# Hybrid S5 and sparse-attention decoder step on one core: layer 1's compression page loads start after layer 0's attention output projection, yields between the key splits, and other ScalarE and GpSimd costs in the emission's model

## The chip, the cores and the metric

One Trainium2 chip, and one of its cores. The time is device microseconds of one execution of the whole program. A profiled execution gives, beside its time, the span from the first to the last instruction and the records of every engine: PE (TensorE matmuls), PEld (TensorE weight loads), DVE (VectorE), ACT (ScalarE), POOL (GpSimd) and SP (SyncE, which issues the DMAs here).

## The reference

Two layers of a parallel-branch trunk work on 512 prompt tokens and on 32 sample tokens (8 sequences of 4), all in float32, D = 1024. Each layer does this:

- modulation: `mod = silu(c) @ ada_w + ada_b`, three parts, `h = rmsnorm(x) * (1 + scale) + shift`;
- one input projection `h @ w_in`, split into the S5 branch, the queries, six key and value groups, gates and merge logits;
- an S5 state-space scan, GELU, a gated linear unit and an output projection;
- sparse attention in three parts. The *compressed* part turns blocks of 64 key or value rows into one row, `silu(blk @ w1) @ w2`; for the sample tokens these rows lie in 128 pages of a paged cache (8 sequences of 16 pages) and have to be fetched by a page table. The *selected* part attends to the best blocks, the *window* part to the last 512 rows;
- `b_nsa = (o * silu(z_nsa)) @ w_nsa_out`, the two branches merged by sigmoid gates, `out = merged @ w_o`, `x = x + gate * out`.

After the second layer one RMSNorm gives the outputs. Layer 1 can't be modulated before layer 0's `x` is complete, but its cache pages and its modulation weights depend on the inputs alone.

## The kernel before

**Arithmetic.** Each big product runs as three matmuls on float32r halves: an operand is split into a rounded copy (`act.copy`, a CAST on ScalarE) and the rest (`sub`, a subtraction on VectorE). A weight tile of 128 x 1024 is fetched by one 512 KB DMA through a ring of three buffers, cast, subtracted and used. One projection of 128 outputs takes 48 matmuls (8 blocks of the input, 3 products, 2 halves of the tokens), one with 512 inputs takes 24.

**Emission.** The program is written as some dozen Python generators (`dense`, `compress`, `prompt`, `sample`, `s5`, `modulation`, page loaders and so on). A scheduler (`_Sched.run`, line 252) picks one of them at each step, lets it emit a few instructions and takes the next; nothing is reordered afterwards. Every engine then executes its own instructions in the order of emission, so an instruction that has to wait holds back all that stand behind it on that engine. The scheduler goes by a model of the engines (`_Clock.note`, line 146), which adds up a cost for each instruction and remembers when each piece of memory is written and read. The model's time of TensorE is the scheduler's clock. A generator yields a delay, a wait for a named event (`ev`), for room in memory, or for the modelled time at which operands are ready. Among those that are ready the lowest number wins: page loaders 4, sample attention 5, compression 15, prompt attention 20, modulation 25, dense 50. So a matmul of the compression goes ahead of the dense work as soon as the *model* holds its pages to be landed.

**ScalarE and GpSimd in the model** (lines 204 to 211). A ScalarE instruction costs 0.051 us where an operand is in PSUM, else 0.093, plus 0.83 ns for each element of a row, plus 0.09 for an accumulator and 0.09 for a bias operand. The same sum is the time for which the engine is held and the time at which its result is visible. A GpSimd operation other than a copy or memset costs 0.27 us plus 2.7 ns an element.

**Between the layers.** When layer 0's attention is complete (event `att`), several generators go on at once:

- `dense` (lines 1103 to 1122) does the attention's output projection, here called *nsa*: eight tiles m of 24 matmuls. Each half tile is merged on VectorE with two spilled arrays, `mn` and `mt`, which `gates(m)` fetches two tiles ahead through three buffers. Then comes the output projection *wo*: eight tiles of 48 matmuls, each with its weight DMA (`in_wo`) and a DMA of old x (`in_xT`), and the root-mean-square of the new x. With event `x` the layer is complete, its normalisation and layer 1's `modulate` follow, and `dense` of layer 1.
- `compress(1)` (line 1612) takes its memory, fetches `cw2`, `cw1` (2 of 1 MB) and `pe4`, and spawns `loads()` (line 1639), which fetches the 128 pages in eight chunks c0 to c7, four pages at a time, 128 KB each (`in_cmp`). There are two chunk buffers: the pages of chunk c wait for the products of chunk c-2. `products` of a chunk are 128 matmuls. From c5 on they wait for event `x` (CMP_LATE = 5), and c7 also for layer 1's own keys.
- `modulation` of layer 1 fetches 24 tiles of `ada_w` of 512 KB in pairs, each pair after the matmuls of the last.

All of these DMAs are issued by SP, in the order of emission.

**Key splits.** `prompt` (line 1705) starts, in each layer, when the input projection and the new compressed rows are there. It first splits the keys: four times a CAST of 64 x 512 and a subtraction of 64 x 512 (lines 1730 to 1734), without a yield between them.

Of the kernel before, what the change touches and what calls it, by code (L numbers as in the profile page):

```python
# [18 lines left out]
PSUM = bass.MemoryType.PSUM  # L19
# [84 lines left out]
class _Clock:  # L104
# [41 lines left out]
    def note(self, e, op, args, kw):  # L146

        named = dict(kw)
        views = [x for x in args if isinstance(x, bass.AP)] + [x for x in named.values() if isinstance(x, bass.AP)]
        if not views:  # L150
            return 0.0
        out = named.get("out", views[0])
        outs = [out] + ([named["accum_out"]] if "accum_out" in named else [])
        ins = [x for x in views if not any(x is y for y in outs)]
        rs, wr = [self.span(x) for x in ins], [self.span(x) for x in outs if not x.tensor.name.startswith("out_")]
        data = max([x[0, c].max() for x, c in rs], default=0.0)
        room = max(x[0 if e != "pe" else 1:, c].max() for x, c in wr) if wr else 0.0
        n = max(x.free_size() for x in views)
        t0 = self.free.get(e, 0.0)
        t0 = max(t0, data + 0.13, room + 0.13 if room > t0 else 0.0)  # L160
        if e == "pe":

            n, rhs, p0 = out.free_size(), views[-1] if op == "matmul" else views[1], out.offset // out.ap[0][0]
            wide = rhs.dtype == F32
            m, k_, r0 = out.ap[0][1], views[1].ap[0][1], views[1].offset // views[1].ap[0][0]
            up = lambda x: 1 if x <= 32 else 2 if x <= 64 else 4
            tile_, passes = (up(k_), up(m)), 2 if wide and op == "matmul" else 1
            load = (0.045 if rhs.dtype == BF16 else 0.111) * up(m) / 4  # L170
            c = 2 * n / 2400 + 0.003 if wide else n / (2400 if rhs.dtype == BF16 else 2180) + 0.002
            if not self.warm(t0):
                c, load = 2 * c, 2 * load
            ready = max(data + 0.15, room + 0.15)
            qs = {(r, q) for r in range(r0 // 32, r0 // 32 + up(k_)) for q in range(p0 // 32, p0 // 32 + up(m))}
            k = int(max(self.free[e], ready) // TICK)
            if passes == 2 and tile_ == self.tile and not qs & self.quads and ready <= self.begun + 0.05:
                self.quads |= qs
                end = self.free[e] + 0.007
            else:  # L180
                if tile_ == self.tile:
                    t0 = max(self.free[e], load + max(self.pass0, ready))
                else:
                    t0 = load + max(self.free[e] + (0.09 if self.tile else 0.0), ready)
                c = max(c, load)
                self.quads, self.tile, self.begun = qs, tile_, t0
                end, self.pass0 = t0 + passes * c, t0 + (passes - 1) * c
            self.ticks[k] = self.ticks.get(k, 0) + n * k_ / P * (1 if not wide else 4 if op == "matmul" else 2)
            self.free[e] = end
            vis = end + 0.07  # L190
        elif op == "dma_start":
            h = self.free[e] = t0 + 0.45
            d = max(self.free.get("dma", 0.0), h + 0.65)
            n = max(x.free_size() * x.ap[0][1] for x in views[:2]) / P if out.space != DRAM else out.free_size() * out.ap[0][1] / P
            end = self.free["dma"] = d + n * 1.42e-3 + 0.01
            vis = end + 0.78
        else:
            extra = 0.061 * sum(1 for x in ins[1:] if x.free_size() == 1) if e == "dve" else 0.0
            if e == "dve":
                far = any(abs(x.ap[-1][0]) >= 8 and x.ap[-1][1] > 1 for x in ins)  # L200
                fast = op in ("tensor_scalar", "tensor_copy", "memset") and all(x.space != PSUM for x in [out] + ins)
                c = 0.155 + extra + n * (0.0063 if op == "reciprocal" else 0.0019 if op == "tensor_tensor_scan" else
                                         0.00055 if fast else 0.0015 if far else 0.001)
            elif e == "act":
                table = {AF.Sin: "sin", AF.Sqrt: "sqrt", AF.Tanh: "exp", AF.Exp: "exp"}.get(args[2] if len(args) > 2 else None)
                if table and table != self.table:
                    t0, self.table = t0 + 1.28, table
                c = (0.051 if any(x.space == PSUM for x in ins) else 0.093) + n * 0.00083 + 0.09 * (
                    ("accum_out" in named) + (isinstance(named.get("bias"), bass.AP)))
            else:  # L210
                c = 0.27 + n * (0.0035 if op == "tensor_copy" else 0.0009 if op == "memset" else 0.0027)
            vis = end = self.free[e] = t0 + c
        for x, c in rs:
            x[1, c] = np.maximum(x[1, c], end)
        for x, c in wr:
            x[0, c] = np.maximum(x[0, c], vis)
        return vis
# [75 lines left out]
def body(ctx: ExitStack, tc: tile.TileContext, A, O):  # L293
# [52 lines left out]
    def t(lat=0.0):  # L346
        return ("t", lat)
# [3 lines left out]
    def ev(*k):  # L351
        return ("ev", k)

    def done(*k):
        S.events[k] = S.ready
# [155 lines left out]
    def sub(dst_lo, src, hi):  # L511
        dve.tensor_tensor(dst_lo, src, hi.bitcast(F32), op=ALU.subtract)
# [13 lines left out]
    def unlag():  # L526
        while lagged:
            sub(*lagged.pop())
# [226 lines left out]
    def dense(l):  # L755
# [352 lines left out]
        for m2 in range(4):  # L1108
            w = wnext(("nsaow", l, m2))
            for m in (2 * m2, 2 * m2 + 1):  # L1110
# [3 lines left out]
                for h, (a, b) in enumerate(HALVES):  # L1114
# [5 lines left out]
                    split_lag(mh(m, a, b), ml(m, a, b), mt(m, a, b))  # L1120
                    yield t()
        unlag()
        for b in mnb:
            b.free()
        for b in q["ogh"] + [q["ogb"]]:
# [440 lines left out]
    def page_ids(i, n=4):  # L1566
        S.clock.free["sp"] = max(S.clock.free.get("sp", 0.0), S.now) + 0.3 + 0.11 * n
        _, v = nc.values_load_multi_w_load_instructions(
            pt[0:1, i:i + n], engines=[mybir.EngineType.SP], min_val=0, max_val=A["cmp"].shape[0] - 1,
            skip_runtime_bounds_check_because="the page table is clamped to the pool on chip")  # L1570
        return v
# [40 lines left out]
    def compress(l):  # L1612
# [24 lines left out]
        done("ckb", l)  # L1637

        def loads():
            for c in range(NB):  # L1640
                if c >= CKB[l]:
                    yield ev("ck", l, c - CKB[l])
                ck = cks[c % CKB[l]]
                for i in range(0, NPG, 4):
                    for j, v in enumerate(page_ids(NPG * c + i)):
                        sp.dma_start(ck[:, i + j].rearrange("p t d c -> p (t d c)"),
                                     A["cmp"][ds(v, 1), l].rearrange("g p f -> (g p) f"))
                    yield t(PG_LAT)
                yield "for", [], [ck[:, 0:NPG + 1]]
                yield t(CK_LATE)  # L1650
                done("ckl", l, c)
        S.spawn(loads(), 4, "ckload")
        if l > 0:
            yield ev("att", l - 1)
        for c in range(NB):
# [15 lines left out]
            n = 84 if last else 64  # L1671
# [33 lines left out]
    def prompt(l):  # L1705
# [24 lines left out]
        for at in range(2):  # L1730
            for g in range(2):
                src = qk(4 + at)[half[g], 0:T]
                act.copy(ks[at][g][half[g]], src)
                sub(ks[at][g][half[1 - g]], src, ks[at][g][half[g]])
            q["qkb"][4 + at].free()

        def queries(qt, r):
# [350 lines left out]
    def main():  # L2088
# [4 lines left out]
        S.spawn(modulation_first([B[6], B[4]]), 2, "ada0")  # L2093
        S.spawn(modulate(0), 3, "h")
        S.spawn(dense(0), 50, "dense")
        yield ev("modq", 0)
        sp.dma_start(pt, A["page_table"])
# [19 lines left out]
        for l in range(DEPTH):  # L2117
            yield ev("qkv", l)
            S.spawn(prompt(l), PR_PRIO, "prompt")
            yield ev("gelu", l, 3)  # L2120
            S.spawn(sample(l), SM_PRIO, "sample")
            if l + 1 < DEPTH:
                yield ev("att", l)
                S.spawn(compress(l + 1), CMP_PRIO, "cmp")
# [229 lines left out]
```

## Time and profile before

| | |
|---|---|
| runs of the kernel | 1247.3 us median of 3 (1238.85 to 1257.79) |
| profiled execution | 1244.75 us |
| its span | 1243.0 us, mean granted TensorE clock 0.967 |
| PE busy | 1142.0 us, 92% |
| PEld busy | 1037.6 us, 83% |
| DVE busy | 780.4 us, 63% |
| ACT busy | 481.5 us, 39% |
| POOL busy | 154.8 us, 12% |
| chain that ended last | PE 69%, DMA 11%, DVE 7%, ACT 4%, SP queue 4% |

Engines work side by side, so the busy shares don't add up. The granted clock is 1 at 2.4 GHz and 0.5 at 1.2 GHz; a mean between them says for how much of a stretch TensorE ran at the lower level. Layer 0 goes up to about 660 us, layer 1 from there.

### The profile page before, as it was taken

The numbers are of one execution on the slowest core, as the hardware profiler recorded it, in microseconds if no ns is written. First come the engines' busy times: TensorE is split into PE (matmuls) and PEld (weight loads), VectorE is DVE, ScalarE is ACT, GpSimd is POOL, SyncE is SP. The second block draws the span as 40 slices with busy tenths as digits, with TensorE's granted clock in tenths as the row PEclk, the third lists the DMA queues.
The fourth block names the chain that finished last, engine by engine and source line by source line (L and its number), as shares of the span: only waits on it lengthen the run. The fifth ranks groups of instructions, "written<-read, shape, count | busy, mean of one in ns | idle before, by whom it ended". The sixth has DMA issues, their size and how long they took to land.

```text
span 1243.0 us, 30351 instructions
## 1 busy us (share of the span) xinstructions
PE 1142.0 (92%) x11702; PEld 1037.6 (83%) x11702; DVE 780.4 (63%) x1787; ACT 481.5 (39%) x1130; POOL 154.8 (12%) x335
## 2 busy tenths in 40 slices
PE   4989999999999999887897999979999899999995
PEld 3788999988888888777885899868898788889995
DVE  4766777566666755763336587797665667556854
ACT  4432432333444444432125233244343444454332
POOL 0122261010000000000002033450010000000001
PEclk9999999999999999988998999989999999999997
DMA  9575666657567655349998744545466665733742
GB/s 386 218 225 180 192 181 187 180 176 245 153 187 237 190 165 170 107 165 294 308 308 262 268 162 133 160 135 142 129 213 197 197 194 167 235 104 97 237 131 81
DMA packets 174434, 239.19 MB, mean 192 GB/s; under 512 B 33233, under 2 KB 129618, under 8 KB 172498
## 3 DMA queue, kind: packets, MB, share of 16 engines
q1 hardware_dynamic: 174290, 237.25, 60.2%
q8 instruction: 92, 1.51, 0.5%
q14 instruction: 52, 0.43, 0.1%
HBM read 207.53 MB, written 37.98 MB: 198 GB/s over the span
## 4 chain that ended last, share of the span: by engine, by line
PE 69%; DMA 11%; DVE 7%; ACT 4%; SPq 4%; issue 2%; POOL 0%; DVEq 0%; ACTq 0%; POOLq 0%
PE bank L231 69%; DVE m L231 7%; SPq L231 3%; ACT m L231 3%; DMA m<-in_cmp 2%; DMA m<-in_cw 2%; DMA yd<-m 1%; DMA m<-in_ada_w 1%; DMA m<-kpd 1%; DMA m<-ud 1%; DMA m<-yd 1%; DMA m<-in_s5k 0%; DMA m<-in_wo 0%; ACT L231 0%; DMA gd<-m 0%
## 5 line engine op out<-in xcount | busy, mean ns | idle before, releaser
L231 PE MATMUL bank<-m,m 128*128 128x256 f32 (+13 forms) x10540 | 1048.2, 283 | 62.5 <-DVE m L231 26.6
L231 PEld LDWEIGHTS bank<-m,m 128*128 128x128 f32 (+4 forms) x10540 | 946.5, 168 | 135.5 <-issue 55.4
L231 DVE TENSOR_TENSOR m<-m,m 128x1024 fp32r<-128x1024 f32 (+15 forms) x635 | 386.2, 630 | 156.8 <-ACT m L231 129.6
L231 ACT CAST m<-m 128x1024 fp32r<-128x1024 f32 (+5 forms) x274 | 174.2, 650 | 89.3 <-DVE m L231 62.8
L231 ACT COPY m<-bank 128x512 f32<-128x512 f32 (+7 forms) x258 | 100.1, 400 | 268.0 <-PE bank L231 258.4
L231 ACT ACTIVATE m<-m 128x544 f32<-128x544 f32 (+8 forms) x74 | 34.7, 476 | 186.0 <-DVE m L231 171.8
L231 POOL TENSOR_TENSOR m<-m,m 128x32 f32<-128x32 f32 (+4 forms) x100 | 57.6, 595 | 327.3 <-DMA x_mid<-m 152.8
L231 PE MATMUL bank<-c_k,m 128*128 128x128 f32 (+2 forms) x590 | 88.8, 277 | 5.0 <-DVE m L231 2.8
L231 ACT ACTIVATE m<-bank 128x288 f32<-128x288 f32 (+4 forms) x130 | 50.4, 390 | 104.5 <-PE bank L231 103.8
L231 POOL CAST m<-m 64x128 fp32r<-64x128 f32 x64 | 23.3, 364 | 505.2 <-ACT m L231 426.5
L231 PEld LDWEIGHTS bank<-c_k,m 128*128 128x128 f32 (+1 forms) x590 | 68.0, 145 | 15.0 <-DVE m L231 5.2
L231 ACT ACTIVATE m<-bank,m 128x128 f32<-128x128 f32 (+4 forms) x132 | 67.8, 523 | 14.4 <-DVE m L231 11.4
L231 DVE TENSOR_REDUCE m<-bank 128x1 f32<-128x128 f32 (+4 forms) x132 | 57.3, 474 | 18.6 <-PE bank L231 17.9
L231 DVE COPY m<-bank 128x32 f32<-128x32 f32 (+6 forms) x102 | 39.1, 389 | 46.4 <-ACT m L231 24.7
L231 DVE SCALAR_TENSOR_TENSOR m<-m,bank 128x256 f32<-128x256 f32 x96 | 41.5, 434 | 41.2 <-ACT m L231 25.1
L231 POOL TENSOR_TENSOR m<-m,c_k 128x256 f32<-128x256 f32 (+2 forms) x32 | 36.0, 1126 | 158.8 <-PE bank L231 136.1
L231 DVE TENSOR_SCALAR m<-m,m,m 128x128 f32<-128x128 f32 (+3 forms) x132 | 52.5, 439 | 2.5
L231 DVE SCALAR_TENSOR_TENSOR m<-m,m 128x64 f32<-128x64 f32 (+5 forms) x64 | 28.9, 480 | 18.5 <-ACT m L231 18.0
L231 ACT ACTIVATE m<-m,m 128x512 f32<-128x512 f32 (+2 forms) x24 | 15.9, 662 | 59.9 <-DVE m L231 59.9
L231 DVE SCALAR_TENSOR_TENSOR m<-bank,mod,m 128x256 f32<-128x256 f32 x32 | 15.4, 482 | 34.9 <-PE bank L231 21.3
L231 DVE TENSOR_TENSOR m<-bank,m 64x16 f32<-64x16 f32 (+1 forms) x56 | 19.8, 385 | 24.4 <-PE bank L231 23.4
L231 ACT ACT_TABLE_LOAD x24 | 30.8, 1283 | 7.1 <-DVE m L231 6.0
(59 smaller groups left out, 397.2 us busy)
## 6 DMA issues: line engine op xcount, KB each, us to landing
m<-in_wblk SPq DMA_DIRECT2D x78, 512.0 KB, 4.1
m<-in_cmp SPq DMA_DIRECT2D x256, 128.0 KB, 3.7
m<-in_kvsel SPq DMA_DIRECT2D x256, 128.0 KB, 3.0
m<-in_ada_w SPq DMA_DIRECT2D x32, 512.0 KB, 5.1
m<-in_ada_q SPq DMA_DIRECT2D x8, 1024.0 KB, 14.7
m<-in_wo SPq DMA_DIRECT2D x16, 512.0 KB, 4.8
ms<-m SPq DMA_DIRECT2D x16, 272.0 KB, 3.3
m<-ms SPq DMA_DIRECT2D x16, 272.0 KB, 3.4
```

The source lines that it names most:

```text
L231: return f(*args, **kw)
```

## The change

The model charges ScalarE 0.074 us more for an instruction with an operand in PSUM and 0.052 us more for any other, and GpSimd 0.4 ns more an element. `dense` sets an event `nsa` when it has emitted the attention's output projection, and the page loader of layer 1 waits for that event of layer 0 ahead of its first page. The four key splits of `prompt` yield 0.4 us after each. No instruction is added, taken out or changed in shape; only the order of emission can differ.

```diff
@@ _Clock.note
-                c = (0.051 if any(x.space == PSUM for x in ins) else 0.093) + n * 0.00083 + 0.09 * (
+                c = (0.125 if any(x.space == PSUM for x in ins) else 0.145) + n * 0.00083 + 0.09 * (
                     ("accum_out" in named) + (isinstance(named.get("bias"), bass.AP)))
             else:
-                c = 0.27 + n * (0.0035 if op == "tensor_copy" else 0.0009 if op == "memset" else 0.0027)
+                c = 0.27 + n * (0.0035 if op == "tensor_copy" else 0.0009 if op == "memset" else 0.0031)
@@ dense
         unlag()
+        done("nsa", l)
         for b in mnb:
             b.free()
@@ compress
         def loads():
+            if l > 0:
+                yield ev("nsa", l - 1)
             for c in range(NB):
@@ prompt
                 act.copy(ks[at][g][half[g]], src)
                 sub(ks[at][g][half[1 - g]], src, ks[at][g][half[g]])
+                yield t(0.4)
             q["qkb"][4 + at].free()
```

## Rows read from the trace of the kernel before

**Rows 1.** The page: busy us, share of the span and instructions of each engine.

```profile
PE 1142.0 (92%) x11702; PEld 1037.6 (83%) x11702; DVE 780.4 (63%) x1787; ACT 481.5 (39%) x1130; POOL 154.8 (12%) x335
```

**Rows 2.** Table of stretches: stretch, its us, busy us (instructions) by engine, clock, DMA, GB/s.

```profile
536.00:700.00 164.00, 138.71 (x1754) 126.97 (x1755) 75.87 (x186) 46.14 (x93) 6.46 (x22) 0.91 0.86 283
557.00:575.00 18.00, 9.66 (x70) 8.71 (x64) 5.83 (x14) 2.62 (x5) 0.00 (x0) 0.81 0.88 287
660.00:700.00 40.00, 29.57 (x401) 26.04 (x402) 22.14 (x65) 16.70 (x40) 6.46 (x22) 0.79 0.82 271
```

**Rows 3.** Timeline of PE after layer 0's attention: start, us, instructions, [idle before, releaser].

```profile
564.81 5.37 PE L231 MATMUL bank<-m,m 128*128 128x256 f32 x24 [5.14 <-DVE m L231]
570.93 1.68 PE L231 MATMUL bank<-m,m 128*128 128x256 f32 x12 [0.75 <-DVE m L231]
574.56 7.21 PE L231 MATMUL bank<-m,m 128*64 128x68 f32 x152 [1.95 <-DMA m<-in_cmp]
595.30 6.45 PE L231 MATMUL bank<-m,m 128*64 128x64 f32 x146 [3.29 <-DMA m<-in_cmp]
...
685.00 8.80 PE L231 MATMUL bank<-m,m 128*64 128x64 f32 x152 [5.32 <-DMA m<-in_ada_w]
```

**Rows 4.** Timeline of DVE, the merge of nsa tile 5.

```profile
564.24 0.42 DVE L231 SCALAR_TENSOR_TENSOR m<-m,bank 128x256 f32<-128x256 f32 x1 [5.65 <-DMA m<-mn]
```

**Rows 5.** Timeline of SP's queue, the same stretch: DMAs in order of issue.

```profile
551.69 3.66 SPq L231 DMA_DIRECT2D m<-in_cmp  x4
557.54 0.33 SPq L231 DMA_DIRECT2D m<-mn  x1
561.53 0.33 SPq L231 DMA_DIRECT2D m<-mt  x1
562.40 4.37 SPq L231 DMA_DIRECT2D m<-in_cmp  x8
...
568.74 1.93 SPq L231 DMA_DIRECT2D m<-in_cmp  x4
```

**Rows 6.** The chain that ended last, ahead of the mt load.

```profile
549.15 12.37 DMA m<-in_cw
```

**Rows 7.** All page loads of layer 1: issue ns, first and last start.

```profile
L231 SPq DMA_DIRECT2D m<-in_cmp x128: 332/333/1791, 551.7 to 697.6; - x128
```

**Rows 8.** Timeline of PE at the products of the last chunk, c7.

```profile
761.54 7.95 PE L231 MATMUL bank<-m,m 128*64 128x84 f32 x172
```

**Rows 9.** Key splits: DVE group of 817 to 836, PE row behind it (layer 1), PE in layer 0.

```profile
L231 DVE TENSOR_TENSOR m<-m,m 64x512 fp32r<-64x512 f32 x4 | 2.7, 685 | 0.1
...
835.39 3.96 PE L231 MATMUL bank<-m,m 128*128 128x256 f32 x28 [5.11 <-DVE m L231]
...
254.84 22.15 PE L231 MATMUL bank<-m,m 128*128 128x256 f32 x213
```

**Rows 10.** ScalarE: four casts in a row, and two groups (busy us, mean ns of one).

```profile
534.14 2.18 ACT L231 CAST m<-m 128x512 fp32r<-128x512 f32 x4 [3.82 <-DVE m L231]
...
L231 ACT CAST m<-m 128x512 fp32r<-128x512 f32 x8 | 4.4, 616 | 5.3 <-DVE m L231 5.3
L231 ACT COPY m<-bank 128x512 f32<-128x512 f32 x64 | 37.5, 586 | 62.4 <-PE bank L231 61.2 <-issue 1.0
```

**Rows 11.** Waits of PE over the whole span, by releaser: us, times, longest.

```profile
PE bank L231 <- ACT m L231: 14.6, 17, 3.3
```

**Rows 12.** Timeline of PE at the end of layer 0's prompt attention.

```profile
517.68 2.22 PE L231 MATMUL bank<-m,m 128*64 128x128 f32 x20 [1.13 <-DVE m L231]
...
521.95 2.21 PE L231 MATMUL bank<-m,m 128*64 128x128 f32 x20 [1.04 <-DVE m L231]
```

**Rows 13.** Behind layer 1's attention: timeline of PE, and of SP's queue.

```profile
1139.76 74.12 PE L231 MATMUL bank<-m,m 128*128 128x288 f32 x594
...
1151.48 0.32 SPq L231 DMA_DIRECT2D mn<-m  x1
```

**Rows 14.** GpSimd: the group of 128 x 256 additions.

```profile
L231 POOL TENSOR_TENSOR m<-m,m 128x256 f32<-128x256 f32 x14 | 13.1, 940 | 123.7 <-ACT m L231 114.9 <-DVE m L231 8.1
```

## The prediction

> **What bounds the kernel now.** First the busy shares: TensorE is busy for 1142.0 of 1243.0 us and no other engine for more than 63% [rows 1]. As the change neither adds nor removes an instruction, TensorE's work stays, and only its idle 101 us and the time at the lower clock can move. The second view is a table of stretches, to find where the idle time lies. Between 536 and 700 us, the passage from layer 0 to layer 1, TensorE is busy for 138.71 of 164 us, so a quarter of all idle time (25.3 us) lies there, at a mean granted clock of 0.91 and with the DMA engines 86% busy at 283 GB/s [rows 2]. Both parts count: 18 us from 557 on hold only 9.66 us of matmuls at 0.81, and 40 us from 660 on hold 29.57 at 0.79 [rows 2].
>
> The timelines say what those stalls wait for. In the attention's output projection TensorE stands 5.14 and then 0.75 us behind VectorE [rows 3], and VectorE had waited 5.65 us for a load of mn [rows 4]. In SP's queue that load stands behind four page loads, is issued at 557.54, and its partner mt only at 561.53 [rows 5], the moment at which the 1 MB of cw1 (549.15 + 12.37) has landed [rows 6]; I read that as a bound on the loads in flight. Then TensorE stands 1.95 us for the pages of chunk c0 and 3.29 us for those of c1, and 5.32 us ahead of a product of 128 x 64 at 685 [rows 3]. The five together are 16.45 of the 25.3 us. The last is named for a modulation load, but the instruction reads pages, so I take it for a page wait too.
>
> **The gate on the pages.** It is a wait of a generator, not of an instruction: no engine stands at it. What moves is SP's order. Sixteen page loads were issued ahead of 571 us (4, 8 and 4) [rows 5]; these and all later ones go behind the mn and mt loads, the first weights of wo and one or two pairs of modulation weights. Four pages occupy SP for 1.93 us [rows 5] and are 0.52 MB, or 1.83 us at the 287 GB/s of that stretch [rows 2].
> - The 5.14 us stall: cw1 stays ahead of mn, so most of it stays. The four pages go: -1.8 us (bounds -5.1 and 0).
> - The 0.75 and 1.95 us: mn of the later tiles no longer queues behind eight pages, and c0's products leave the projection: -2.7 us (bounds -2.7 and 0).
> - c0's products come later, with their own wait on pages in a full DMA queue. Nearest rows 1.95 and 3.29: I take +2.0 (bounds 0 and +3.3). c1's 3.29 stays.
> - Clock: 0.81 over 18 us means the lower level for 38%, 6.8 us. With some 2.5 us less stall I take -1.0 (bounds -3.4, half of 6.8, and 0).
> - The page stream: 128 pages from 551.7 to 697.6 are 1.15 us a page [rows 7]. Starting about 22 us later it would end near 720 at the same pace. The products of c7 run at 761.54 [rows 8], so its pages have cover of 64 us; if that were gone, c7 would hold TensorE by the difference. c3 to c6 have the wo loop and layer 1's first projections beside them. The modulation weights gain what the pages lose, as both share the DMA engines. I take 0 here (bounds -5.3, the wait at 685 gone, and +10.6, it and another of its size added).
>
> Sum of the gate: -1.8 - 2.7 + 2.0 - 1.0 = -3.5 us.
>
> **The yields.** In layer 1 the four subtractions are 4 x 0.685 = 2.74 us in one piece on VectorE, and a few microseconds on TensorE stands 5.11 us behind VectorE [rows 9]. With yields dense evacuations can go between them. VectorE's whole backlog there is longer than these four, so I take half: -1.4 us (bounds -2.7 and +0.7, one subtraction, if prompt's start slips). In layer 0 TensorE runs 213 matmuls through the same place without a stall [rows 9]: 0.
>
> **ScalarE in the model.** Single instructions last longer than the model said: a 128 x 512 cast has 616 ns [rows 10] against 0.093 + 0.425 = 0.518, now 0.570; a copy from PSUM 586 ns [rows 10] against 0.476, now 0.550. But four casts in a row took 2.18 us [rows 10], not 4 x 0.616 = 2.46, so each starts 0.094 us before the last one ends, and the pace is (2.18 - 0.616) / 3 = 0.521 us, the old figure. The new one is the better delay and the worse pace. For delays, TensorE waits 14.6 us on ScalarE in all [rows 11]; if later emission puts other work into a third of that, -5. For pace, a prompt unit holds two exponentials and a copy from PSUM and, on average, one cast: 3 x 0.074 + 0.052 = 0.27 us later by the model, 8.8 us over the 32 units of a layer. In layer 0 dense work has run out by 517 us; units then follow at 521.95 - 517.68 = 4.27 us, each with TensorE idle for some 1.1 us [rows 12]. Two units more without cover (8.8 / 4.27) cost 2.2 us. In layer 1 TensorE runs on without a gap when attention ends at about 1139.8, and the last spilled array mn is stored at 1151.48 [rows 13]: some 11 us of dense work were still left, cover for the 8.8 us. I take +1.0 (bounds -5 and +4.4, two layers of 2.2).
>
> The Trainium skill, "ScalarE: Activation LUTs", section "What ACT_TABLE_LOAD costs", puts an instruction with immediate operands at 186 ns plus 0.833 ns an element and says: "Back-to-back ACTIVATEs overlap by ≈ 93 ns." The trace agrees, with 94 ns. By that rule 186 - 93 is the model's old 0.093, and the change charges the engine for time in which it already works on the next instruction; it speaks against this part.
>
> **GpSimd in the model.** A 128 x 256 addition takes 940 ns [rows 14]; the old model had 961, the new 1064. These lie in the key and query rotation, which nothing reads before the attention starts: 0 (bounds -0.5 and +0.5, half an addition).
>
> **Sum.** -3.5 - 1.4 + 1.0 + 0 = -3.9 us. The profiled execution took 1244.75 us, 1.75 beyond its span and 2.5 below the median of the three runs (1247.3, themselves 1238.85 to 1257.79). 1244.75 - 3.9 = 1240.9: I forecast **1241 us**.
>
> **Rivals.**
> - *The waits only move.* DMA engines that are 86% busy over 164 us [rows 2] have 46 MB to bring whatever the order. If the time saved in the projection returns as waits of c0 to c6, the gate is worth 0; with yields and ScalarE 1244.75 - 0.4 = **1244.4**. For it: the waits at 574.56, 595.30 and 685 are all for such loads. Against: outside the two worst stretches 106 us hold only 6.5 us of idle time (25.3 - 8.3 - 10.4), with the DMA engines as busy.
> - *Late pages (the slower side).* It decides whether c5 and c6 land before the normalisation of x and the first half of layer 1's modulation are over. Their products are emitted ahead of dense work once the model holds them landed, so a late chunk holds layer 1's first projections. Two more waits of 5.32 us [rows 3] and nothing gained by the gate: 1244.75 + 10.6 - 0.4 = **1255**. For it: 22 us of delay, and the wait at 685 exists already. Against: modulation, which shares the queue, is done earlier.
> - *ScalarE overcharged.* The attention of both layers is emitted later and loses its dense cover: +4.4 in place of +1.0, 1240.9 + 3.4 = **1244.3**. For it: the 0.094 us overlap; against: the 11 us of cover in layer 1. It is the page's rule above.
> - *The passage clears.* The whole 16.45 us but the 3.3 that cw1 keeps go, and half of the clock's loss (1.7) comes back: 1244.75 - 13.2 - 1.7 - 0.4 = **1229.5**. For it: one cause may stand behind all five stalls. Against: the DMA share.
>
> **How the numbers follow.** Chances: forecast 0.45, waits move 0.20, late pages 0.12, ScalarE overcharged 0.10, passage clears 0.13. The likeliest case alone spans 1234 to 1247, the sum with half of its bounds. The range has to reach to 1229.5 and to 1255, and the runs of this kernel differ by some 10 us from their median, so I put it at 1226 to 1257. Two per cent, about what a measurement of this kernel tells from no change, are 25 us: faster than 1222 needs the last case with more than I found, 0.06; slower than 1272 needs the late pages with several more waits, 0.03; within, 0.91.
>
> **What would show it.** The page loads start behind 565 us in SP's queue and the mn loads stand ahead of them; the stall of 5.14 us is 3 to 4 and those of 0.75 and 1.95 inside the projection are gone; the first wo weight lands earlier; the last page loads are issued later than 697.6; the 5.11 us stall in layer 1 is shorter; the idle time of the passage falls from 25.3 to about 22 us. I am wrong if the mn wait vanishes altogether (cw1 was not its cause), if new waits on pages stand at layer 1's first projections, or if layer 0's attention ends more than 3 us later, counted from the last dense work of its layer.

## The result, and the profile after

Slower by 1.1%: 1260.6 us (median of 4 runs, 1257.7 to 1261.7) against 1247.7 of the kernel before beside it; the ratio is 1.011, interval 1.0075 to 1.0145. The profiled execution took 1261.2 us with a span of 1259.4. The forecast of 1241 and its range, 1226 to 1257, both miss. An execution far slower than the others of its kernel (one of x17 took 1573.6 us at a granted clock of 0.649, two of x16 were over 1.5% above its fastest) is left out of the ratios below, and of the medians of x16 and x17.

The page of the kernel after: busy us of TensorE, which answers to [rows 1]. It ran the same 11702 matmuls and was busy for 11.5 us longer.

```profile
PE 1153.5 (92%) x11702; PEld 1046.4 (83%) x11702; DVE 774.0 (61%) x1787; ACT 485.6 (39%) x1134; POOL 157.9 (13%) x335
```

The table of stretches after, the same three as in [rows 2]. The passage between the layers holds 138.61 us of matmuls, as before (138.71): what the 18 us from 557 on won (13.74 against 9.66, clock 0.93 against 0.81) is not in the sum of the 164 us, whose idle time is 25.4 us where I had expected some 22.

```profile
536.00:700.00 164.00, 138.61 (x1741) 125.67 (x1742) 75.03 (x182) 49.30 (x96) 5.91 (x22) 0.91 0.82 275
557.00:575.00 18.00, 13.74 (x103) 12.56 (x96) 11.24 (x25) 5.48 (x11) 0.00 (x0) 0.93 0.92 359
660.00:700.00 40.00, 30.71 (x503) 27.08 (x504) 18.31 (x53) 13.18 (x34) 4.73 (x19) 0.77 0.83 274
```

SP's queue after, in order of issue, beside [rows 5]: no page load stands between the mn and mt loads, and the first pages go out at 574.26 in place of 551.69. The second fence is the group of all page loads, from 574.3 to 708.8 in place of 551.7 to 697.6 [rows 7].

```profile
553.28 0.33 SPq L231 DMA_DIRECT2D m<-mn  x1
553.94 0.33 SPq L231 DMA_DIRECT2D m<-mt  x1
554.32 0.89 SPq L231 DMA_DIRECT2D m<-in_cw  x2
...
556.49 0.39 SPq L231 DMA_DIRECT2D m<-mn  x1
...
558.68 0.33 SPq L231 DMA_DIRECT2D m<-in_wo  x1
...
574.26 4.38 SPq L231 DMA_DIRECT2D m<-in_cmp  x8
```

```profile
L231 SPq DMA_DIRECT2D m<-in_cmp x128: 332/333/1887, 574.3 to 708.8; - x128
```

TensorE's stalls in the passage after, beside [rows 3]. Of the 5.14 us behind an mn load 1.56 are left. The 2.50 at 571.08 are another wait, for the split of the first wo weight, which was issued at 558.68 and took 9.57 us to land. The wait of 5.32 at 685 is gone; two page waits (662.36 and 675.67) stand just ahead of layer 1's first projections.

```profile
566.89 1.68 PE L231 MATMUL bank<-m,m 128*128 128x256 f32 x12 [1.56 <-DVE m L231]
571.08 8.61 PE L231 MATMUL bank<-m,m 128*128 128x288 f32 x54 [2.50 <-DVE m L231]
589.32 1.66 PE L231 MATMUL bank<-m,m 128*128 128x256 f32 x12 [1.62 <-DVE m L231]
...
613.93 3.95 PE L231 MATMUL bank<-m,m 128*64 128x64 f32 x128 [2.15 <-DMA m<-in_ada_w]
...
662.36 6.46 PE L231 MATMUL bank<-m,m 128*64 128x64 f32 x128 [2.40 <-DMA m<-in_cmp]
...
675.67 8.24 PE L231 MATMUL bank<-m,m 128*64 128x64 f32 x140 [2.45 <-DMA m<-in_cmp]
```

To say where the time went, I cut each execution at the last store of x_mid in SP's queue, where layer 0's result is complete: at 663.0 us before and 656.6 after. The two halves before, then after (columns as in [rows 2]):

```profile
0.00:663.00 663.00, 602.38 (x6602) 542.14 (x6602) 395.71 (x906) 247.71 (x573) 71.43 (x165) 0.97 0.67 213
663.00:1243.00 580.00, 539.66 (x5101) 495.49 (x5101) 384.64 (x881) 233.76 (x558) 83.33 (x170) 0.96 0.54 169
```

```profile
0.00:656.60 656.60, 598.09 (x6463) 537.67 (x6463) 392.05 (x906) 250.08 (x575) 80.50 (x165) 0.98 0.65 210
656.60:1259.40 602.80, 555.39 (x5239) 508.76 (x5239) 381.97 (x882) 235.52 (x559) 77.37 (x170) 0.94 0.54 168
```

Layer 0 is complete 6.4 us earlier, layer 1 takes 22.8 us more. 139 matmuls have moved from the first half to the second: most of it one chunk's 128 products of pages, 3.95 us long, as the row at 613.93 shows. Without that move it would be some 2.5 us won and 19 lost. In layer 1 both kinds of loss are there: 7.1 us more idle time (47.4 against 40.3), and 15.7 us more busy time, 3.95 of them the moved chunk, at a mean clock of 0.94 instead of 0.96.

### The profile page after: what moved, and what is told of

It reads as the page before. It is cut to its first block, busy times and chain, and to the rows that moved or that the text cites. A ratio compares the mean times of both kernels' runs of the same rounds, so it can differ in the third digit from the quotient of the medians.

```text
span 1259.4 us, 30375 instructions
## 1 busy us (share of the span) xinstructions
PE 1153.5 (92%) x11702; PEld 1046.4 (83%) x11702; DVE 774.0 (61%) x1787; ACT 485.6 (39%) x1134; POOL 157.9 (13%) x335
## 2 busy tenths in 40 slices
DMA packets 174434, 239.19 MB, mean 190 GB/s; under 512 B 33233, under 2 KB 129618, under 8 KB 172498
## 4 chain that ended last, share of the span: by engine, by line
PE 67%; DMA 11%; DVE 10%; ACT 4%; SPq 4%; issue 3%; POOL 0%; DVEq 0%; ACTq 0%; POOLq 0%
PE bank L231 67%; DVE m L231 10%; ACT m L231 4%; SPq L231 4%; DMA m<-ud 2%; DMA m<-in_xT 2%; DMA m<-in_ada_q 1%; DMA m<-kpd 1%; DMA m<-in_cmp 1%; DMA m<-in_wo 1%; DMA m<-in_s5k 1%; DMA m<-in_nsaow 1%; ACT L231 1%; DMA kpd<-m 0%; POOL m L231 0%
## 5 line engine op out<-in xcount | busy, mean ns | idle before, releaser
L231 PE MATMUL bank<-m,m 128*128 128x256 f32 (+11 forms) x10540 | 1060.8, 284 | 69.4 <-DVE m L231 33.8
L231 PEld LDWEIGHTS bank<-m,m 128*128 128x128 f32 (+3 forms) x10540 | 957.1, 169 | 145.7 <-issue 48.7
L231 DVE TENSOR_TENSOR m<-m,m 128x1024 fp32r<-128x1024 f32 (+13 forms) x635 | 385.5, 630 | 163.1 <-ACT m L231 144.8
L231 ACT CAST m<-m 128x1024 fp32r<-128x1024 f32 (+7 forms) x274 | 174.2, 650 | 85.7 <-DVE m L231 53.9
L231 ACT ACTIVATE m<-m 128x64 f32<-128x64 f32 (+7 forms) x74 | 34.8, 476 | 171.1 <-DVE m L231 162.3
L231 ACT ACTIVATE m<-bank 128x256 f32<-128x256 f32 (+5 forms) x130 | 50.6, 390 | 91.2 <-PE bank L231 90.3
L231 DVE TENSOR_SCALAR m<-m,m,m 128x128 f32<-128x128 f32 (+4 forms) x132 | 52.6, 441 | 2.5
L231 DVE TENSOR_TENSOR m<-bank,c_k 128x256 f32<-128x256 f32 (+5 forms) x52 | 16.7, 322 | 33.4 <-PE bank L231 33.3
```

The costliest lines, as they stand in the source:

```text
L231: return f(*args, **kw)
```

## The experiments

Each kernel ran beside the kernel before, whose own median moved between 1241.7 and 1247.7 from one set of runs to the next, so the ratio is what compares. "x complete" is the cut above in the profiled execution, "rest" its span behind the cut; that is one execution, up to 11 us off the median of its kernel. "Costs" are the model's ScalarE constants (PSUM and SBUF source): 0.051 and 0.093 old, 0.125 and 0.145 new.

```
run                        gate yields costs           us      ratio (interval)         x complete  rest
before                      -    -    old              1245.4  1                           663.0   580.0
after                       x    x    new              1260.6  1.0110 (1.0075..1.0145)     656.6   602.8
x1_scalar_only              -    -    new              1283.1  1.0291 (1.0234..1.0349)     683.8   598.4
x2_gate_only                x    -    old              1230.8  0.9885 (0.9848..0.9922)     645.7   579.6
x3_all_but_scalar           x    x    old              1236.3  0.9918 (0.9884..0.9952)     655.4   586.4
x4_all_but_gate             -    x    new              1268.5  1.0177 (1.0121..1.0233)     677.2   594.5
x5_delay_only               x    x    new, delay only  1267.1  1.0193 (1.0158..1.0227)     667.3   605.7
x6_pace_only                x    x    new, pace only   1264.1  1.0160 (1.0107..1.0212)     674.5   588.0
x7_half                     x    x    half way         1269.1  1.0202 (1.0156..1.0248)     664.7   607.0
x8_minus_half               x    x    below the old    1261.9  1.0142 (1.0102..1.0183)     660.4   602.5
x9_plus_2ns                 x    x    old + 2 ns       1256.1  1.0111 (1.0075..1.0148)     663.4   588.6
x10_minus_2ns               x    x    old - 2 ns       1252.1  1.0065 (1.0043..1.0087)     649.4   600.8
x11_vector_2ns              x    x    old, VectorE + 2 1249.4  1.0047 (1.0020..1.0073)     651.6   597.6
x12_gate_plus_2ns           x    -    old + 2 ns       1261.9  1.0156 (1.0111..1.0202)     647.7   607.8
x13_no_gate_plus_2ns        -    -    old + 2 ns       1261.7  1.0116 (1.0039..1.0192)     668.0   591.0
x14_yields_plus_2ns         -    x    old + 2 ns       1258.4  1.0112 (1.0089..1.0135)     668.9   581.7
x15_after_vector_2ns        x    x    new, VectorE + 2 1265.8  1.0143 (1.0073..1.0213)     683.7   589.1
x16_after_minus_2ns         x    x    new - 2 ns       1251.6  1.0015 (0.9968..1.0062)     648.5   605.5
x17_scalar_from_layer1      x    -    new in layer 1   1260.9  1.0123 (1.0082..1.0165)     648.2   600.4
x18_yields_layer1           x    l1   old              1233.0  0.9899 (0.9864..0.9933)     648.8   582.5
```

**Which part.** x1 and x2 put one part each into the kernel before; x3 and x4 take one part each out of the kernel after.

```diff
# x1, and undone in x3
-                c = (0.051 if any(x.space == PSUM for x in ins) else 0.093) + n * 0.00083 + 0.09 * (
+                c = (0.125 if any(x.space == PSUM for x in ins) else 0.145) + n * 0.00083 + 0.09 * (
# x2, and undone in x4
+        done("nsa", l)
...
+            if l > 0:
+                yield ev("nsa", l - 1)
```

> The kernel before with nothing but the new ScalarE costs in the emission's model; no gate, no yields, GpSimd as before. Theory A (the ScalarE costs reorder the attention of both layers so that dense work runs out early, 2.6 us at the end of layer 0's attention and more at the end of layer 1's): nearly the whole loss is here, 1256 to 1260 us. Theory B (the gate makes the pages late and layer 1's first projections with them, first matmul at 684.84 against 674.40): 1247 to 1251. Theory C (no single part: each reorders the emission and costs a little): 1250 to 1254.

> The kernel before with nothing but the gate on layer 1's pages. Theory A: the gate is worth nothing or gains a little, 1243 to 1248 us, and the wait behind the mn load is gone. Theory B: 1255 to 1260, with layer 1's first projections some 10 us later. Theory C: 1250 to 1254.

> The kernel after with the old ScalarE costs put back (gate, yields and the GpSimd cost stay). Theory A: the loss is undone, 1243 to 1248 us. Theory B: 1256 to 1260. Theory C: 1252 to 1256.

> The kernel after without the gate (new ScalarE and GpSimd costs and the yields stay). Theory A: the loss stays, 1257 to 1262 us. Theory B: 1247 to 1251. Theory C: 1253 to 1257.

Theory A holds in sign, and all its sizes are too small: the gate alone gains 14.6 us, the ScalarE costs alone lose 37.7, and without them the other parts gain 9. Theories B and C fall with x2, which both had slower than the kernel before. The way from before to after is 1245.4, gate 1230.8, yields 1236.3, ScalarE 1260.6; the GpSimd cost is no step of it, since with gate and yields the emission with the old GpSimd cost and with the new one is the same instruction by instruction on every engine.

In the trace of the gate alone the stall of 5.14 us is 3.29, those of 0.75 and 1.95 are gone, and the products of chunk c1 wait 2.52 at 609.47 (3.29 before). Those of c0 run between 584.8 and 594.6 without a wait (last row, a group of instructions). The third row is taken up under the yields.

```profile
560.46 12.89 PE L231 MATMUL bank<-m,m 128*128 128x256 f32 x90 [3.29 <-DVE m L231]
...
609.47 3.95 PE L231 MATMUL bank<-m,m 128*64 128x64 f32 x128 [2.52 <-DMA m<-in_wo]
...
809.96 2.84 PE L231 MATMUL bank<-m,m 128*128 128x256 f32 x22 [1.86 <-DVE m L231]
...
L231 PE MATMUL bank<-m,m 128*64 128x68 f32 x128 | 4.0, 223 | 0.0
```

**Delay, pace or size.** x5 keeps only the later end of a result, x6 only the later free time of the engine (one of the two added lines in each); x7 and x8 change the size.

```diff
             vis = end = self.free[e] = t0 + c
+            if e == "act":
+                self.free[e] = end - (0.074 if any(x.space == PSUM for x in ins) else 0.052)    # x5
+                vis = end = end - (0.074 if any(x.space == PSUM for x in ins) else 0.052)       # x6
...
+                c = (0.088 if any(x.space == PSUM for x in ins) else 0.119) + n * 0.00083 + 0.09 * (    # x7
+                c = (0.014 if any(x.space == PSUM for x in ins) else 0.067) + n * 0.00083 + 0.09 * (    # x8
```

> The kernel after, with the longer ScalarE durations used only for when a result can be read; the engine's own free time goes by the old costs. Between the run without the ScalarE costs (1236) and the kernel after (1260). Theory P (pace: consecutive instructions overlap by 0.094 us, so the old cost was the engine's pace and the loss comes from holding the engine busy too long): 1234 to 1242 us. Theory D (delay: each chain through ScalarE is emitted later and dense work goes ahead of it): 1256 to 1262.

> The kernel after, with the longer ScalarE durations used only for when the engine is free again; a result can be read by the old costs. Theory P: 1256 to 1262 us. Theory D: 1234 to 1242.

> The kernel after with half of the addition to the ScalarE costs (0.088 and 0.119). If the loss grows with the cost (theories P and D): 1244 to 1252 us. If any change of the emission scatters the time (theory S): anything from 1230 to 1270, with no order among the doses.

> The kernel after with ScalarE costs lowered by half of the addition (0.014 and 0.067, below the old ones). Theories P and D: the chains are emitted earlier, 1224 to 1238 us, no slower than the run with the old costs (1236). Theory S: above it, 1240 to 1265.

Theories P and D both fall. Half of the addition costs no less than the whole (1269), and costs below the old ones lose as well (1262), where both wanted a gain. The losses do not sit in one place either. In x5 TensorE stands 12.25 us behind x complete, before most of layer 1's first projections: the products of two chunks are emitted while their pages are still in flight. This is the rival of the late pages, in a kernel that differs from x3 by ScalarE's delays alone. TensorE's timeline of x5:

```profile
682.34 6.32 PE L233 MATMUL bank<-m,m 128*64 128x64 f32 x128 [10.04 <-DMA m<-in_cmp]
...
698.51 3.95 PE L233 MATMUL bank<-m,m 128*64 128x64 f32 x128 [2.21 <-DMA m<-in_cmp]
```

**Two nanoseconds.** A change of 2 ns is no better or worse as a duration, but the emission that follows from it is another one.

```diff
-                c = (0.051 if any(x.space == PSUM for x in ins) else 0.093) + n * 0.00083 + 0.09 * (
+                c = (0.053 if any(x.space == PSUM for x in ins) else 0.095) + n * 0.00083 + 0.09 * (    # x9, x12
+                c = (0.049 if any(x.space == PSUM for x in ins) else 0.091) + n * 0.00083 + 0.09 * (    # x10
-                c = 0.155 + extra + n * (0.0063 if op == "reciprocal" else 0.0019 if op == "tensor_tensor_scan" else
+                c = 0.157 + extra + n * (0.0063 if op == "reciprocal" else 0.0019 if op == "tensor_tensor_scan" else    # x11
```

> All but the ScalarE costs (gate, yields, GpSimd; 1236 us), with every ScalarE cost of the model raised by 2 ns (0.053 and 0.095), too little to mean anything for a real duration, but the emission parts from that of the base behind its first 948 groups of TensorE instructions. Theory S (the emission of the base is one lucky draw, and any redraw of it loses): 1255 to 1270 us. Theory L (what loses is a ScalarE cost that is off by tens of ns, either way): 1230 to 1243.

> The same base with every ScalarE cost lowered by 2 ns (0.049 and 0.091); the emission parts from the base behind its first 317 groups of TensorE instructions. Theory S: 1255 to 1270 us. Theory L: 1230 to 1243.

> The same base with every VectorE cost raised by 2 ns and the ScalarE costs as they were. Theory S: 1255 to 1270 us. Theory L: 1230 to 1243.

> The gate alone (1231 us) with every ScalarE cost raised by 2 ns: a second base. Theory S: 1250 to 1265 us. Theory L: 1225 to 1238.

None of the four lands where theory L wants it: they lose 20, 16, 13 and 31 us against their bases. Theory S has the sign, and two of the four in its range; x10 and x11 are milder. But its "any redraw of it loses" can't hold as it stands: x2 and x3 are redraws of the kernel before as well, by the gate and the yields, and both are faster than it. In x11 the place is again a chunk ahead of layer 1's first projections:

```profile
666.23 5.90 PE L231 MATMUL bank<-m,m 128*64 128x64 f32 x128 [8.71 <-DMA m<-in_cmp]
```

**More draws, with and without the gate.** x13 is x12 without the gate, x14 is x9 without it; x15 and x16 are the kernel after with 2 ns more on VectorE or less on ScalarE.

```diff
# x13 (x12 without the gate), x14 (x9 without the gate)
-            if l > 0:
-                yield ev("nsa", l - 1)
# x15
-                c = 0.155 + extra + n * (0.0063 if op == "reciprocal" else 0.0019 if op == "tensor_tensor_scan" else
+                c = 0.157 + extra + n * (0.0063 if op == "reciprocal" else 0.0019 if op == "tensor_tensor_scan" else
# x16
-                c = (0.125 if any(x.space == PSUM for x in ins) else 0.145) + n * 0.00083 + 0.09 * (
+                c = (0.123 if any(x.space == PSUM for x in ins) else 0.143) + n * 0.00083 + 0.09 * (
```

> The kernel before with every ScalarE cost raised by 2 ns: the run of the gate with plus 2 ns (1262 us) without its gate. Theory G (the gate itself gains, about 8 to 15 us in any emission): 1268 to 1278 us. Theory R (the gate's gain was a luck of that one emission): within 5 of 1262, or below it.

> Yields, GpSimd cost and plus 2 ns on ScalarE, without the gate: the run of all but the ScalarE costs with plus 2 ns (1256 us) without its gate. Theory G: 1263 to 1272 us. Theory R: within 5 of 1256, or below it.

> The kernel after with every VectorE cost of the model raised by 2 ns: another emission around the full ScalarE costs. Theory S (only the redraw loses, whatever the costs): as the draws of 2 ns around the old costs, 1249 to 1262 us. Theory L2 (the full costs lose some 10 us beyond a redraw): 1262 to 1275.

> The kernel after with the new ScalarE costs lowered by 2 ns (0.123 and 0.143): one more emission around the full costs. Theory S: 1249 to 1262 us. Theory L2: 1262 to 1275.

With the gate, the four emissions from old costs moved by 2 ns have a mean ratio of 1.0095 (x9 to x12), the three from the new costs, as they are or moved by 2 ns, 1.0089 (after, x15, x16). So with the gate nothing shows that the new ScalarE costs lose by their size: theory L2 finds x15 on its side and x16 against it, and the means are equal. Without the gate the new costs stand at 1.0291 and 1.0177 (x1, x4) and the costs moved by 2 ns at 1.0116 and 1.0112 (x13, x14), some 8 to 22 us apart. With two emissions on each side, whether the size of the costs adds to the loss stays open.

The gate's end result is not robust: its four pairs differ by -14.6 us (before, x2), -8 (x4, after), 0 (x13, x12) and -2 (x14, x9); by the ratios -14, -8, +5 and 0. Theory R is right on the whole time, theory G on the passage. In all four pairs the gate shortens the time from the last load of key and value rows in layer 0 (the last in_kvsel load in SP's queue, up to which the emission of a pair is the same) to x complete: 192.7 to 179.6, 182.1 to 168.5, 184.2 to 164.4 and 191.5 to 179.9 us. These are single executions: up to that load the two of a pair, with the same emission, differ by 0.5 to 7 us. The rest changes by -0.4, +8.3, +16.8 and +6.9: layer 1 is emitted anew behind the gate.

**One layer, and the yields where the forecast put them.** x17 and x18 stand on the gate alone and leave its emission of layer 0 as it is.

```diff
# x17
+    late = 0
...
         done("nsa", l)
+        S.clock.late = 1
...
-                c = (0.051 if any(x.space == PSUM for x in ins) else 0.093) + n * 0.00083 + 0.09 * (
+                c = (0.051 if any(x.space == PSUM for x in ins) else 0.093) + (0.074 if any(x.space == PSUM for x in ins) else 0.052) * self.late + n * 0.00083 + 0.09 * (
# x18
                 sub(ks[at][g][half[1 - g]], src, ks[at][g][half[g]])
+                if l > 0:
+                    yield t(0.4)
```

> The gate alone (1231 us), with the new ScalarE costs in the model only from the end of layer 0's attention output on; the emission of layer 0 is the gate's. If each redrawn layer loses its own share: layer 0 as in the gate's run (x complete at about 646 us) and 8 to 18 us lost in layer 1, 1239 to 1249. If the loss sits in layer 0's front: 1226 to 1235.

> The gate alone with the yields between the key splits of layer 1 only. The forecast's step (dense evacuations go between the subtractions): -1.4 us, so 1229 to 1230, and the stall behind VectorE at the start of layer 1's attention on the prompt shortens from 5.1 to some 3.7 us. If what counts is that layer 1 is redrawn from there: 1234 to 1248, whatever that stall does.

x17 misses both expectations: layer 0 is as in x2 (648.2 and 645.7), and layer 1 alone loses 30 us by the medians, 21 in the profiled executions (x17's is its fastest). So the loss is not tied to layer 0's front. The pair shows what such a loss is made of. The stretches from x complete, from the load of s5k, from the first and the last load of in_kvsel in layer 1, and from the last mn load to the end, first of x2, then of x17:

```profile
645.70:674.10 28.40, 18.79 (x255) 15.05 (x251) 17.01 (x44) 13.01 (x33) 6.08 (x22) 0.76 0.85 290
674.10:901.70 227.60, 215.34 (x2148) 201.50 (x2146) 169.52 (x365) 85.59 (x191) 68.09 (x122) 0.98 0.54 170
901.70:1074.30 172.60, 169.35 (x1654) 149.91 (x1654) 111.76 (x289) 79.23 (x219) 6.93 (x20) 1.00 0.63 198
1074.30:1150.60 76.30, 76.30 (x749) 69.77 (x748) 46.35 (x101) 33.66 (x79) 0.70 (x2) 1.00 0.50 162
1150.60:1225.30 74.70, 59.40 (x463) 58.34 (x462) 40.41 (x89) 24.35 (x42) 3.79 (x4) 0.93 0.38 123
```

```profile
648.20:676.20 28.00, 18.44 (x265) 14.63 (x260) 17.00 (x44) 12.97 (x33) 6.07 (x22) 0.76 0.90 300
676.20:910.70 234.50, 212.49 (x2120) 199.88 (x2121) 169.12 (x361) 87.61 (x191) 57.09 (x113) 0.96 0.53 166
910.70:1083.10 172.40, 163.71 (x1619) 143.31 (x1618) 111.23 (x291) 77.27 (x216) 8.68 (x29) 0.99 0.60 184
1083.10:1172.10 89.00, 88.45 (x818) 82.02 (x818) 49.20 (x103) 37.00 (x83) 0.70 (x2) 1.00 0.53 164
1172.10:1248.60 76.50, 62.30 (x463) 61.11 (x461) 39.13 (x88) 24.57 (x42) 3.44 (x4) 0.88 0.37 121
```

Of 20.8 us, 14.6 are idle time: 9.7 in the second stretch (22.0 against 12.3), 5.4 in the third, less 0.6 in the other three. The other 6.2 are busy time, as in the last stretch, where the same 463 matmuls take 62.30 us at a clock of 0.88 and 59.40 at 0.93. The two largest stalls of x17's second stretch have no partner over 2.6 us in x2:

```profile
834.82 6.22 PE L232 MATMUL bank<-m,m 128*128 128x256 f32 x36 [5.91 <-DVE m L232]
...
872.66 5.89 PE L232 MATMUL bank<-m,m 128*128 128x288 f32 x32 [4.77 <-DVE m L232]
```

x18 is 2 us above x2, with intervals that overlap: neither the -1.4 of the forecast nor a loss of 4 or more is seen. The stall behind VectorE at this place was 1.86 us in x2 already, without any yield (the row at 809.96 above). With the yields it is 1.33, and a wait for ScalarE follows. TensorE's timeline of x18:

```profile
813.72 2.88 PE L231 MATMUL bank<-m,m 128*128 128x256 f32 x22 [1.33 <-DVE m L231]
...
837.61 1.11 PE L231 MATMUL bank<-c_k,m 128*128 128x128 f32 x4 [3.61 <-ACT m L231]
```

## Why the prediction was wrong

**The step that failed is "ScalarE in the model", +1.0 us with bounds of -5 and +4.4.** Between x3 and the kernel after it is worth +24 us, of which 13 to 20 are what moving one cost by 2 ns took from the same x3 (x9 to x11). The working took the emission as one fixed order in which the prompt units slide by 8.8 us a layer, and asked what covers them. But the model's clock decides at every step which generator goes next, so a new constant gives another order from the first instructions on, with other overlaps everywhere. The runs show it: x7 to x12 lose 13 to 33 us against their bases with half of the addition, with lower costs, or with costs 2 ns off, and x5 and x6 lose as much by the delays alone as by the pace alone. The bounds therefore could not come from a count of slipped units; they had to come from how much emissions of this kernel differ.

The mechanism that the working did name, dense work that runs out before the attention ends, is there in layer 0, and larger than the two units I counted. The last row of dense matmuls ends at 515.5 before (511.53 + 3.97), at 520.9 in x3 (517.74 + 3.19) and at 483.6 in the kernel after (481.01 + 2.62, first row). From there to the end of the attention TensorE is idle for 7.5 of 21.6 us before, 8.3 of 21.2 in x3 and 13.6 of 56.1 after (the three rows of stretches, in this order):

```profile
481.01 2.62 PE L231 MATMUL bank<-m,m 128*128 128x288 f32 x18
...
515.50:537.10 21.60, 14.07 (x121) 10.66 (x118) 11.50 (x23) 8.66 (x20) 0.00 (x0) 0.88 0.19 64
520.90:542.10 21.20, 12.86 (x120) 9.63 (x117) 12.27 (x25) 8.72 (x21) 0.11 (x1) 1.00 0.19 65
483.60:539.70 56.10, 42.54 (x469) 31.05 (x467) 36.47 (x88) 27.05 (x71) 2.10 (x6) 0.96 0.30 90
```

But layer 0 gets those 5 us back elsewhere: up to x complete TensorE is idle for 58.5 us in the kernel after and for 60.1 in x3. In these two executions the loss is in layer 1. From the first in_kvsel load of layer 1 to the last mn load, x3 (first fence) has 2.2 us of idle time, the kernel after (second fence) 12.8:

```profile
921.30:1165.40 244.10, 241.86 (x2366) 215.29 (x2366) 158.30 (x395) 112.47 (x295) 8.92 (x30) 1.00 0.59 185
```

```profile
930.80:1184.90 254.10, 241.28 (x2291) 213.02 (x2292) 156.22 (x386) 107.94 (x284) 9.95 (x31) 0.97 0.57 173
```

Half of it are three stalls in the middle of the attention, where I had not looked. One stands at its start, behind GpSimd, and 3.3 us stand at its end, where I had counted on 11 us of dense work as cover:

```profile
936.89 5.18 PE L231 MATMUL bank<-m,m 128*32 128x32 f32 x32 [2.97 <-POOL m L231]
...
995.67 0.66 PE L231 MATMUL bank<-c_k,m 128*128 128x128 f32 x4 [1.62 <-ACT m L231]
...
1001.27 6.51 PE L231 MATMUL bank<-m,m 128*128 128x256 f32 x62 [1.95 <-ACT m L231]
...
1013.28 9.64 PE L231 MATMUL bank<-m,m 128*128 128x256 f32 x52 [2.91 <-DVE m L231]
...
1163.55 0.39 PE L231 MATMUL bank<-m,m 128*128 128x256 f32 x1 [1.43 <-ACT m L231]
1165.84 24.44 PE L231 MATMUL bank<-m,m 128*128 128x256 f32 x175 [1.90 <-DVE m L231]
```

**The gate** (-3.5) had SP's order right and its size too small. In x2 the 5.14 us stall is 3.29 (I had 3.3), and those of 0.75 and 1.95 are gone (-2.7). That the first figure fits is partly luck: I had the loads held back in SP's queue, mn behind the pages and mt until cw1 landed. In x2 the mn load goes out at 549.08, ahead of the stall, and then takes 10.72 us to land (a row of the chain that ended last):

```profile
549.08 10.72 DMA m<-mn
```

The wait of c0's products, for which I took +2.0, did not come, and c1's is 2.52 in place of 3.29. The pages end at 704.4 in x2 and 708.8 after, ahead of the 720 I gave them, and c7's products still find theirs landed. From the last in_kvsel load of layer 0 to x complete the gate won 11.6 to 19.8 us in the four pairs, or some 8 to 12 without the products that moved behind it (by the counts of matmuls one chunk, 3.95 us, in three pairs, and two in x12). What I had at 0 is gone too, the wait of 5.32 at 685 [rows 3]; behind x complete x2 waits 3.20 and 0.94 us for pages instead (at 660.95 and 676.66). The rival that came nearest for the gate alone is "the passage clears", 1229.5 against 1230.8 measured, in its number more than in its mechanism, as those two waits show. In the other pairs layer 1 gave back 7 to 17 us, for which my working had no term.

**The yields** (-1.4): alone in layer 1 within 2 us of nothing (x18); in both layers +5.5 (x3 against x2), part of which must be layer 0's order, which I had at 0, if x18's 2 us are layer 1's share. In the kernel after, the place of the 5.11 us [rows 9] shows two stalls that sum to 4.58:

```profile
838.34 4.62 PE L231 MATMUL bank<-m,m 128*128 128x256 f32 x24 [1.95 <-DVE m L231]
845.59 4.61 PE L231 MATMUL bank<-m,m 128*128 128x288 f32 x22 [2.63 <-DVE m L231]
```

**GpSimd** (0): right, the emission does not change.

**The rival "ScalarE overcharged"** pointed to the right part with the wrong reason. By the rule of the Trainium skill, "ScalarE: Activation LUTs", section "What ACT_TABLE_LOAD costs", the old constant for a source in SBUF is the engine's pace and the new one overcharges it. The trace bears that out for casts of 128 x 512 [rows 10], but not for all: four casts of 64 x 128 in a row, of 0.294 us each, take 1.24 us in the kernel before, with no overlap (ScalarE's timeline, below). If the overcharge were the cause, the delay alone (x5) would be free and only the pace (x6) would lose; they took 1267 and 1264 us. The rule may be true of the engine, and it decides nothing here.

```profile
270.37 1.24 ACT L231 CAST m<-m 64x128 fp32r<-64x128 f32 x4
```

**The signs.** Of my signs of being wrong, two came: page waits ahead of layer 1's first projections (2.40 and 2.45 us), and layer 0's attention, which ended 56.1 us behind the last dense work in place of 21.6, where 3 us more were the mark. The wait for mn did not vanish. And the span of 1234 to 1247 for the likeliest case does not follow from half of the bounds: added up, these give some 1230 to 1253.

**"The change neither adds nor removes an instruction"** was nearly so: ScalarE loads four more tables (groups before and after, busy us and mean ns), 5.1 us on an engine that is idle for 61% of the span. x4 has 24 of them and is slow, x3 has 28 and is fast, so they are not the cause.

```profile
L231 ACT ACT_TABLE_LOAD x24 | 30.8, 1283 | 7.1 <-DVE m L231 6.0 <-PEq L2338 0.7
```

```profile
L231 ACT ACT_TABLE_LOAD x28 | 35.9, 1283 | 15.9 <-DVE m L231 14.8 <-PEq L2342 0.7
```

**What stays open** is why the emissions of the kernel before, of x2, x3 and x18 are 13 to 38 us better than the others, with the gate and without it alike. It is not that they were not redrawn: x2, x3 and x18 are emitted anew from some point on, by the gate or the yields. What the sixteen slower kernels have in common is a cost of ScalarE or VectorE that is not the old one, in x17 only behind layer 0's attention output. No run tests whether the old costs had themselves been kept because their emission was a fast one. Whether the four share one overlap that the others lack was not found; the losses lie in different stretches (x5 and x11 ahead of layer 1's projections, the kernel after in its attention, x15 in layer 0).

## What to carry to other kernels

Where an order is computed by a greedy model, price a change of the model's numbers by a control first: the same kernel with a constant moved by 2 ns shows how far the order alone moves the time, and an edit worth less than that can't be judged from one emission. Judge a part such as the gate by the stretch it acts on and in several emissions, not by the end of the span alone. Of the emissions measured, the one to keep is the gate alone with the old costs: 1230.8 us, 0.9885 of the kernel before (0.9848 to 0.9922), and 30 us below the kernel after.

## What the runs showed of the hardware that was not expected

Idle time came with more than its own length, in the one pair where the two were told apart. Behind x complete, x17 has 14.6 us more idle time than x2 and also 6.2 us more busy time, at a mean granted clock of 0.95 against 0.97, that is with a larger share of its span at the lower of the two levels, 1.2 GHz. And in the passage between the layers, where the DMA engines were 86% busy before [rows 2], the gate took stalls away (0.75 and 1.95 us, and 1.85 of the 5.14) without taking away a byte, with 239.19 MB moved before and in x2: there the order of the loads, and not only what they bring, had set them.
